# Prefix sums on the diagonal of a 2D prefix sum: two column groups moved from TensorE to VectorE, an early fp32 load, and smaller last pieces

## The chip, the cores and the metric

One core of one Trainium2 chip. The metric is device time in microseconds (us). The kernel before takes 668.2 us (median of 6 runs, 667.48 to 669.82).

## The reference

```python
def setup_inputs():
    B, H, W = 4, 4224, 4224
    return {"x": np.random.randn(B, H, W).astype(np.float32)}

def reference(x):
    ps = np.cumsum(np.cumsum(x, axis=1), axis=2)
    diag = np.diagonal(ps, axis1=1, axis2=2)
    return np.cumsum(diag, axis=1).astype(np.float32)
```

Output n is the sum, over diagonal positions up to n, of everything above and left of that position. Every element is read once: 285 MB of fp32 (the page has 285.47 MB read), which the loads cast to bf16 on the way into SBUF (142.47 MB as the software queue wrote them).

## The kernel before

Rows come in strips of 768 (6 per partition) through three buffers. Columns are cut into 11 groups of 384. For a strip, TensorE adds up the columns right of the diagonal block (matmuls with a one-hot column, into `d`), VectorE masks the diagonal block and adds up rows left of it, ScalarE takes a share of those. In the first three batches VectorE adds up one group instead in four of the strips (`by_rows`, result in `rowed`). `rows` are the sums per row; a matmul that reads them adds them to `d`, along which VectorE then runs two scans (prefix sums). A fold is a run of matmuls with the identity, which adds up column pieces on TensorE. The granted clock is the share of TensorE's full clock that the trace records. Cuts are marked `# ...`.

```python
head = last.tile([P, 2, HC], FP32, name="head")          # HC = 528
nc.sync.dma_start(out=head, in_=src_a[:, :, N - HC : N])  # before all strips
# ...
def add_up(strip, f, r0, acc, um, wp=0, ws=None, by_rows=False):
    # ...
    for j in range(g + nw + by_rows, NG):
        for q in range(f):
            columns(j, 0, GW, strip[:, q, j * GW : (j + 1) * GW], q > 0)
    # ...
    nc.vector.tensor_mul(out=mu, in0=block, in1=um)
    nc.vector.tensor_sub(out=block, in0=block, in1=mu)
    if by_rows:
        rowed = mup.tile([P, GW], FP32, name="rowed")
        row_sums(rowed, strip[:, :, hi : hi + GW].rearrange("p q c -> p c q"))
    # ... matmuls on mu, and one on rowed
    row_sums(acc[:, :, 1], strip[:, :, ws:hi])
# ... the last batch ends in two three-row strips, 256 rows (part_a), then
# 128 rows (part_b) in pieces of 32, the last of these in two pieces:
for sb, c0, c1 in ((0, 0, CB), (1, 0, CB), (2, 0, CB), (3, 0, bcut), (3, bcut, CB)):
    nc.gpsimd.dma_start(out=part_b[:, sb, c0:c1], in_=...)
# ... per piece a sum on ScalarE and one on VectorE (pair_sum), weighed by TensorE
pair_sum(esum[:, 1:2], part_b[:, 3, 320:bcut])
pair_sum(esum[:, 2:3], part_b[:, 3, bcut:])
# ...
nc.vector.tensor_add(out=ye, in0=fin_e, in1=yl[:, E0:])
nc.sync.dma_start(out=out[b, T0 + E0 : N].unsqueeze(0), in_=ye)
```

## Time and profile before

| | before |
|---|---|
| span of the profiled run | 665.6 us |
| TensorE, VectorE, ScalarE busy | 206.6, 380.8, 136.1 us |
| loads that go through the software queue | 142.47 MB as written, 99.9% of 16 engines' span |
| instruction fetches of 16 KB | 7 |
| last strip landed (TensorE starts on it) | 648.81 us |
| last sum on VectorE starts | 662.69 us |

The table's first four rows are the profile page; the last two are start times in the timeline. The lines themselves are in the prediction. Where this text speaks of single DMA packets (their queue, size, start and duration), these are records of the trace that no view prints; an engine is recognised in them only by its back-to-back packets, it has no name.

### The profile page before, as it was taken

The page shows a single profiled execution, that of the slowest core. Times are in us where ns is not written, and L with a number is a line of the kernel's source. Part 1 is how long each engine was busy: PE and PEld are TensorE (multiplying, and loading weights), DVE is VectorE, ACT ScalarE, POOL GpSimd, SP SyncE. Part 2 cuts the span into 40 slices and gives each one's busy share as a digit, 9 for nine tenths or more (in the row PEclk, how much of TensorE's full clock was granted, in tenths as well). Part 3 has the DMA queues.
Part 4 walks back from the last instruction along what each step waited for, and adds up shares of the span by engine and source line. Part 5 has one row for each costly group of instructions (what it writes and reads, how often), then busy time and mean ns, then how long its engine had stood idle before and what let it go on. Part 6 is the DMA issues. An engine that isn't in the chain of part 4 may idle for free.

```text
span 665.6 us, 2495 instructions
## 1 busy us (share of the span) xinstructions
PE 206.6 (31%) x948; PEld 94.1 (14%) x948; DVE 380.8 (57%) x176; ACT 136.1 (20%) x219; POOL 31.3 (5%) x59
## 2 busy tenths in 40 slices
PE   0071522302117143140211723404031363350418
PEld 0030211100003021010000311201000131120103
DVE  3161828476946173756794526466589433352766
ACT  0001121406300103040630020304063002030434
POOL 7000000000000000000000000000000000001000
PEclk9995857656558585665655857657565585776758
DMA  9999999999999999999999999999999999999998
GB/s 203 219 219 219 219 219 218 218 209 210 219 220 219 218 220 219 218 216 215 209 219 219 219 216 219 219 218 216 213 213 219 219 216 216 219 218 218 215 206 162
DMA packets 7672, 143.23 MB, mean 215 GB/s; under 512 B 704, under 2 KB 1004, under 8 KB 2156
## 3 DMA queue, kind: packets, MB, share of 16 engines
q0 software_dynamic: 7296, 142.47, 99.9%
q1 hardware_dynamic: 364, 0.61, 0.3%
q8 instruction: 7, 0.11, 0.1%
q14 instruction: 5, 0.04, 0.0%
HBM read 285.47 MB, written 0.07 MB: 429 GB/s over the span
## 4 chain that ended last, share of the span: by engine, by line
DVE 54%; another core or an unknown queue 37%; DMA 5%; PE 3%; issue 1%; DVEq 0%; POOLq 0%
DVE acc L258 28%; DVE mu L351 8%; DVE strip L352 8%; DVE rowed L258 7%; DMA strip<-in_x_dram 5%; DVE c L481 1%; PE d L211 1%; PE fold L218 0%; PE d L218 0%; DVE pu L258 0%; DVE c L278 0%; DVE rows L403 0%; DVE acc L376 0%; PE fold_a L218 0%
## 5 line engine op out<-in xcount | busy, mean ns | idle before, releaser
L253 ACT ACTIVATE dump<-strip 128x416 bf16<-128x416 bf16 (+6 forms) x108 | 124.4, 1151 | 520.2 <-DMA strip<-in_x_dram 517.5
L351 DVE TENSOR_TENSOR mu<-strip,um 128x4608 bf16<-128x4608 bf16 (+1 forms) x24 | 52.4, 2184 | 260.4 <-DMA strip<-in_x_dram 260.3
L258 DVE TENSOR_REDUCE acc<-strip 128x6 f32<-128x4608 bf16 (+6 forms) x23 | 195.9, 8518 | 0.4
L218 PEld LDWEIGHTS <-sel 128*11 128x11 bf16 x643 | 66.7, 104 | 482.5 <-issue 453.6
L211 PE MATMUL d<-strip,sel 128*11 128x384 bf16 x90 | 37.3, 415 | 295.8 <-DMA strip<-in_x_dram 295.8
L218 PE MATMUL d<-strip,sel 128*11 128x384 bf16 x441 | 116.6, 408 | 0.0
L352 DVE TENSOR_TENSOR strip<-strip,mu 128x4608 bf16<-128x4608 bf16 (+1 forms) x24 | 52.4, 2183 | 1.0
L211 PE MATMUL d<-mu,sel 128*11 128x384 bf16 x43 | 16.3, 379 | 108.5 <-DVE mu L351 108.5
L258 DVE TENSOR_REDUCE rowed<-strip 128x384 f32<-128x2304 bf16 x12 | 49.0, 4082 | 0.0
L218 PE MATMUL d<-mu,sel 128*11 128x384 bf16 x200 | 46.7, 369 | 0.0
L76 POOL DMA_DIRECT2D strip<-in_x_dram x24 | 16.4, 686 | 542.7 <-DVE acc L258 292.8
L253 ACT ACTIVATION_READ_ACCUMULATOR dump<-strip 128x1 f32 x108 | 20.1, 186 | 0.0
L211 PE MATMUL d<-rowed,sel_f 128*11 128x384 f32 x24 | 11.5, 566 | 20.3 <-DVE rowed L258 20.3
L211 PEld LDWEIGHTS <-sel 128*11 128x11 bf16 x134 | 13.6, 102 | 19.3 <-issue 12.3
L211 PE MATMUL d<-ident,rows 128*11 128x128 f32 x24 | 5.2, 379 | 16.8 <-DVE rows L412 16.8
L258 DVE TENSOR_REDUCE pu<-d 11x1 f32<-11x384 f32 x4 | 2.2, 545 | 6.3 <-PE d L211 6.3
L94 DVE MEMSET um<- 128x4608 bf16 (+1 forms) x2 | 4.9, 2458 | 1.1 <-issue 1.1
L95 POOL TENSOR_SCALAR_AFFINE_SELECT um<-um 128x4608 bf16<-128x4608 bf16 (+1 forms) x2 | 5.2, 2612 | 2.6 <-DVE um L94 2.6
L211 PE MATMUL d<-halves,rows 128*11 128x64 f32 x48 | 5.3, 288 | 0.0
L211 PEld LDWEIGHTS d<-ident,rows 128*11 128x11 f32 x24 | 2.5, 118 | 18.9 <-DVE rows L412 11.7
L211 PEld LDWEIGHTS d<-rowed,sel_f 128*11 128x11 f32 x24 | 1.5, 91 | 24.9 <-DVE rowed L258 24.6
L211 PEld LDWEIGHTS d<-halves,rows 128*11 128x11 f32 x48 | 4.8, 128 | 1.4 <-issue 1.3
(102 smaller groups left out, 60.6 us busy)
## 6 DMA issues: line engine op xcount, KB each, us to landing
strip<-in_x_dram POOLq DMA_DIRECT2D x19, 6336.0 KB, 72.6
strip<-in_x_dram POOLq DMA_DIRECT2D x5, 3168.0 KB, 55.8
strip<-in_x_dram POOLq DMA_DIRECT2D x1, 1080.0 KB, 49.9
strip<-in_x_dram POOLq DMA_DIRECT2D x1, 768.0 KB, 52.9
strip<-in_x_dram POOLq DMA_DIRECT2D x3, 256.0 KB, 54.1
head<-in_x_dram SPq DMA_DIRECT2D x1, 528.0 KB, 3.8
strip<-in_x_dram POOLq DMA_DIRECT2D x1, 192.0 KB, 43.2
strip<-in_x_dram POOLq DMA_DIRECT2D x1, 64.0 KB, 28.5
```

Of the source, the lines that this page charges most:

```text
L76: nc.gpsimd.dma_start(out=o, in_=x[b, r0 : r0 + f * P, :].rearrange("(p f) w -> p f w", f=f))
L94: nc.vector.memset(um, 1.0)
L95: nc.gpsimd.affine_select(out=um, in_=um, compare_op=ALU.is_gt, fill=0.0, base=0, pattern=[[-1, f], [1, f * P]], channel_multiplier=-f,)
L211: nc.tensor.matmul(o, lhsT=lhsT, rhs=rhs, start=start, stop=False, skip_group_check=True)
L218: te.add_instruction(mybir.InstMatmult(start_tensor_calc=False, stop_tensor_calc=False, tile_position=(0, 0), tile_size=(P, P if lhsT.shap ...
L253: nc.scalar.activation(out=dump[:, :w], in_=src, func=ACT.Copy, accum_out=acc)
L258: nc.vector.reduce_sum(out=acc, in_=src, axis=AX.X)
L351: nc.vector.tensor_mul(out=mu, in0=block, in1=um)
L352: nc.vector.tensor_sub(out=block, in0=block, in1=mu)
L481: nc.vector.tensor_tensor_scan(out=c12[:, i, :], data0=ones_row, data1=src, initial=carry[:, i : i + 1], op0=ALU.mult, op1=ALU.add,)
```

## The change

Its intent: (1) take the two rightmost groups, 9 and 10, off TensorE for all six-row strips: VectorE adds them up in one fp32 tile per batch (a wide add has 768 columns, a narrow one, in the fifth strip of the first three batches, 384), so that TensorE reads only two fp32 tiles per batch; (2) make the end shorter: half of the last 16 rows is loaded right after `head`, before all strips, with an access pattern of outer size 8 meant for 8 DMA engines, and the last loads are three pieces of 131 KB of fp32; (3) issue the store of the groups after the next one. The core of the diff:

```diff
+    early = last.tile([P, EC], FP32, name="early")          # RE = 16, EC = 256
+    nc.sync.dma_start(out=early,
+        in_=src_e.rearrange("(a b) (k c) -> a b k c", b=2, k=EK)[:, :, :, :EC])
...
-            for j in range(g + nw + by_rows, NG):
+            for j in range(g + nw, RJ if right else NG):     # RJ = NG - 2
...
-            if by_rows: rowed = ...; row_sums(rowed, ...)    # and its matmul
+            if right:                                        # after row_sums(acc)
+                c0 = max(hi, RJ * GW)
+                to = right_cols[:, c0 - RJ * GW :]
+                for q in range(f):
+                    if r0 == 0 and q == 0:
+                        continue
+                    nc.vector.tensor_add(out=to,
+                        in0=to if r0 + q > 1 else strip[:, 0, c0:],
+                        in1=strip[:, q, c0:])
...
-            add_up(..., um6, by_rows=whole and s > 0)
+            add_up(..., um6, right=True)
...
+        for j in range(RJ, NG):
+            matmul(d, sel_f[...], right_cols[:, (j - RJ) * GW : (j - RJ + 1) * GW])
...
-   (3, 0, bcut), (3, bcut, CB)
+   for i, (src, c) in enumerate(((src_e, EC), (src_l, 0), (src_l, EC))):
+       nc.gpsimd.dma_start(out=late[:, i * EC : (i + 1) * EC], in_=src...[:, :, c : c + EC])
...
+        store_groups()      # now after the store of yl; one shared tile for pair_sum
```

## The prediction

> **What bounds the kernel now.** I read the slices of the page first, then the waits, the chain in order of time, and last the timeline of the final 30 us.
>
> ```profile
> DVE  3161828476946173756794526466589433352766
> DMA  9999999999999999999999999999999999999998
> GB/s 203 219 219 219 219 219 218 218 209 210 219 220 219 218 220 219 218 216 215 209 219 219 219 216 219 219 218 216 213 213 219 219 216 216 219 218 218 215 206 162
> ```
>
> The 16 DMA engines are busy in nine tenths of every slice but the last, VectorE (DVE) in no long stretch. The kernel is one stream of loads. The waits, where the columns are total us, times and the longest, agree:
>
> ```profile
> POOL strip L76 <- DVE acc L258: 292.8, 9, 35.3
> ...
> DVE mu L351 <- DMA strip<-in_x_dram: 260.3, 20, 20.0
> ```
>
> VectorE waits 260 us for strips. GpSimd (POOL) waits for VectorE to free a buffer, but with three buffers that costs nothing: in the chain (start, us, what) six-row strips reach VectorE every 29.9 us, and it is done some 7 to 20 us before the next.
>
> ```profile
> 454.24 2.57 DVE mu L351
> 456.83 2.56 DVE strip L352
> 459.39 4.00 DVE rowed L258
> 463.39 11.26 DVE acc L258
> 474.65 9.39 another core or an unknown queue
> 484.09 0.04 issue
> 484.13 2.57 DVE mu L351
> ```
>
> The trace's records of single DMA packets say why the stream can't be hurried: a 25344-byte strip packet takes 1886 ns on its engine, and the next starts 1867 ns after it. So only three things count: work per DMA engine, what lies idle at the start, and what follows the last landing. The end of the timeline (start, us, engine, line, operation) is therefore the part to know:
>
> ```profile
> 624.12 11.35 DVE L258 TENSOR_REDUCE acc<-strip 128x6 f32<-128x10752 bf16 x1
> ...
> 635.58 0.18 DVE L376 TENSOR_TENSOR acc<-acc 128x24 f32<-128x24 f32 x1
> ...
> 643.63 0.17 DVE L420 COPY rows<-acc 128x3 f32<-128x3 f32 x1
> ...
> 648.86 0.76 DVE L351 TENSOR_TENSOR mu<-strip,um 128x1152 bf16<-128x1152 bf16 x1 [5.05 <-DMA strip<-in_x_dram]
> ...
> 654.47 0.17 DVE L258 TENSOR_REDUCE rows<-parts 128x3 f32<-128x9 f32 x1
> ...
> 655.36 0.83 PE L211 MATMUL d<-ident,rows 128*11 128x128 f32 x6
> ...
> 658.88 1.00 DVE L481 TENSOR_TENSOR_SCAN c<-ones_row,carry,c 11x384 f32<-11x384 f32 x1
> ...
> 662.35 0.39 DVE L267 SCALAR_TENSOR_TENSOR pair<-strip 128x224 f32<-128x224 bf16 x1
> ...
> 662.69 0.29 DVE L267 SCALAR_TENSOR_TENSOR pair<-strip 128x128 f32<-128x128 bf16 x1
> ```
>
> From 648.86 VectorE works almost without a pause: its only slack ahead of the end is 5.05 us before the last strip, and 0.72 us on TensorE (PE) between rows (done 654.64) and the matmul that reads it (655.36), which stands behind a fold. The last load's completion writes go out at 661.95 to 662.35 and the last pair_sum starts at 662.69, so DMA and VectorE end nearly together.
>
> [...] the 64-column fp32 add at L137 took 225 ns [...], the bf16 multiply of 4608 columns 2558 ns [...]. [...] The trace names no engine, but the 10-row store did go out as 10 packets. [...] each engine's first strip packet starts at 3.74 to 4.27 us, right as its last packet of head ends.
>
> **Part 1, groups 9 and 10 on VectorE.** Removed: 12 reductions `rowed` of 4.08 us, 49.0 us. Added: [...] A batch has 5+6+6+6 = 23 wide ones, the first three batches 6 narrow ones as well. [...] VectorE goes from 380.8 to about 430 us. TensorE loses 138 of 531 strip matmuls (instruction lists of both), at 0.41 us 57 us. In mid-stream neither shows: the busiest strip takes VectorE 5.1 + 11.3 + 6.0 = 22.4 us of 29.9. In the last batch, though, nothing is removed, since `rowed` was not used there. Its fourth strip now ends at 635.54 + 6.0 = 641.5. The three-row strip after it took from 635.58 to 643.80, 8.2 us, so it ends at 649.8, and VectorE meets the last strip (648.86) 0.9 us late. rows is then done at 655.55, the matmul starts 0.14 us later (the lag in earlier batches: 187.07 to 187.21), at 655.68 for 655.36. Of 0.9 us, 0.3 come through. From there to the last pair_sum VectorE is a chain.
>
> **Part 2, early load and last pieces.** All engines lose 8 packets of 1536 B (0.119 us apart) and 8 of 512 B (0.045) and gain 24 of 512 B and one completion of 0.02: 1.31 us to 1.10, -0.2 us at the end. Eight engines gain 16 packets of 1 KB fp32, an estimated 0.042 us each from 2112 B in 0.082: +0.7 us. As head already keeps each engine busy until its first strip packet, this is not hidden at the start; it is hidden only on engines that end early. In the packet records seven end by about 661.3 and nine at 662.0 to 662.35; the slow ones each appear to have carried a 16 KB instruction fetch (0.95 us). Of the ten packets of the row store four go out only at 661.97 to 662.31, on late engines. [...] There the end moves by -0.2 + 0.7 = +0.5 at worst, by +0.1 for the earliest of them. If fetches fall elsewhere in the changed kernel, it is -0.2.
>
> **Part 3, the rest.** The later store removes one 0.08 us packet from an engine's tail at most. The first of the last pieces to VectorE shrinks from 0.39 to 0.29 us; one shared pair tile makes each wait for the one before, about +0.08. These cancel. The sums for weights and earlysum fall in the idle first 34 us.
>
> **Sum.** VectorE's chain ends +0.3 us, the loads between -0.2 and +0.5; the later counts: about +0.3 on 668.14, so 668.4.
>
> **Rivals.** (a) The loads alone set the end, and the early bytes are hidden on the fast engines: -0.2 to -0.3 us, 667.9. For it: the intent, and DMA at nine tenths. Against: VectorE's last start is set by its own predecessor as closely as by the landing. (b) The early load sits on late engines and pushes every landing: +0.5, 668.6. For it: the four late store packets. Against: no record names the engine. (c) VectorE becomes the bound: 50 us more, buffers come free late, the stream stalls, several us (675). Against: at least 7 us idle remain per strip, and a freed buffer's load queues behind a whole other strip. (d) The 57 us less of TensorE speed the kernel: no, it waits 296 us for strips.
>
> **Range and chances.** The terms are tenths of a us; the three runs before span 0.7 us, and another chip or another placing of fetches can add as much. So 667.4 to 669.2. 2% is 13.4 us, which nothing here reaches: faster 0.01, same 0.98, slower 0.01.
>
> **What would show it.** Right: wide adds near 0.96 us; VectorE near 430 us busy; TensorE near 150; strips 29.9 us apart; VectorE meeting the last strip some 0.9 us late with no wait before it; scans and the last pair_sum some 0.3 us later than before. Wrong: a wait before the last strip's multiply (adds cheaper than reckoned), a last landing that moves by over 0.6 us either way, or strips further apart, which would mean that buffers come free too late.

## The result, and the profile after

The changed kernel takes 668.48 us (median of 6, 667.85 to 670.04), the kernel before in the same rounds 668.2. The ratio is 1.0005 with a 95% interval of 0.999 to 1.0021. Here and below a ratio is the mean time of one kernel's fast runs over that of the other's fast runs in the same rounds, so it is not quite the ratio of the medians. The times alone do not settle the sign.

The slices of the page, for the changed kernel, show the same stream of loads with a fuller VectorE (431.0 us busy):

```profile
DVE  3280929486948193857793827476689463765896
DMA  9999999999999999999999999999999999999998
```

The groups by form (line, engine, operation, tiles, shapes, count, then busy us and mean ns of one) have the adds at 957 and 556 ns:

```profile
L396 DVE TENSOR_TENSOR right_cols<-right_cols,strip 128x768 f32<-128x768 f32 x88 | 84.2, 957 | 2.6
L396 DVE TENSOR_TENSOR right_cols<-right_cols,strip 128x384 f32<-128x384 f32 x18 | 10.0, 556 | 0.5
```

In mid-stream the chain (start, us, what) still has 7 us of waiting behind the longest strip:

```profile
471.78 0.88 DVE right_cols L396
472.65 0.02 issue
472.68 0.97 DVE right_cols L396
...
477.61 7.07 another core or an unknown queue
484.68 0.03 issue
```

And the end of the timeline:

```profile
635.99 5.92 DVE L396 TENSOR_TENSOR right_cols<-right_cols,strip 128x768 f32<-128x768 f32 x6
...
649.36 0.36 PE L237 MATMUL fold<-strip,ident_h 128*128 128x480 bf16 x1 [2.38 <-DMA strip<-in_x_dram]
649.95 0.76 DVE L380 TENSOR_TENSOR mu<-strip,um 128x1152 bf16<-128x1152 bf16 x1
...
655.56 0.17 DVE L284 TENSOR_REDUCE rows<-parts 128x3 f32<-128x9 f32 x1
655.78 0.83 PE L237 MATMUL d<-ident,rows 128*11 128x128 f32 x6 [0.38 <-DVE rows L284]
...
663.14 0.29 DVE L294 SCALAR_TENSOR_TENSOR pair<-strip 128x128 f32<-128x128 bf16 x1
```

The six adds of the last batch's fourth strip are there, 5.92 us where 6.0 was reckoned. VectorE takes up the last strip (649.95) with no wait in front, 0.59 us after it landed (649.36, when TensorE starts on it). The strip itself landed 0.55 us later than before. The matmul that reads `rows` comes 0.42 us later than before and now waits for VectorE. The last sum is 0.45 us later, the last store's issue 0.42 (664.03 for 663.61). With the one shared pair tile the last sum starts 0.04 us after the end of the one before it (662.81 + 0.29 to 663.14); with a tile each it started 0.05 us ahead of that end (662.35 + 0.39 to 662.69).

So two things moved by half a us: the landings, and VectorE against the landing. The experiments ask which of them the end pays for, and how much of it is scatter.

### The profile page after: what moved, and what is told of

Its sections match the earlier page's. It is cut to its first block, busy times and chain, and to the rows that moved or that the text cites. A ratio compares the mean times of both kernels' runs of the same rounds, so it can differ in the third digit from the quotient of the medians.

```text
span 666.4 us, 2314 instructions
## 1 busy us (share of the span) xinstructions
PE 180.7 (27%) x804; PEld 81.7 (12%) x804; DVE 431.0 (65%) x279; ACT 136.1 (20%) x219; POOL 32.1 (5%) x62
## 4 chain that ended last, share of the span: by engine, by line
DVE 57%; another core or an unknown queue 27%; DMA 13%; issue 1%; PE 1%; POOL 0%; ACT 0%; DVEq 0%; POOLq 0%; ACTq 0%
DVE acc L284 27%; DVE right_cols L396 14%; DMA strip<-in_x_dram 13%; DVE mu L380 7%; DVE strip L381 7%; DVE c L517 1%; PE d L237 1%; DVE pu L284 0%; DVE c L305 0%; POOL strip L474 0%; POOL strip L478 0%; DVE rows L441 0%; ACT dump L279 0%; DVE acc L409 0%
## 5 line engine op out<-in xcount | busy, mean ns | idle before, releaser
L244 PEld LDWEIGHTS <-sel 128*11 128x11 bf16 x528 | 56.3, 107 | 457.4 <-issue 435.7
L237 PE MATMUL d<-strip,sel 128*11 128x384 bf16 x67 | 28.7, 428 | 308.4 <-DMA strip<-in_x_dram 308.4
L396 DVE TENSOR_TENSOR right_cols<-right_cols,strip 128x768 f32<-128x768 f32 (+1 forms) x106 | 94.2, 889 | 3.2
L244 PE MATMUL d<-strip,sel 128*11 128x384 bf16 x326 | 89.4, 420 | 0.0
L244 PE MATMUL d<-mu,sel 128*11 128x384 bf16 x200 | 49.8, 388 | 0.0
L237 PE MATMUL d<-mu,sel 128*11 128x384 bf16 x43 | 16.7, 389 | 82.0 <-DVE mu L380 82.0
L237 PE MATMUL d<-right_cols,sel_f 128*11 128x384 f32 x16 | 10.9, 793 | 59.6 <-DVE right_cols L396 59.6
L237 PEld LDWEIGHTS <-sel 128*11 128x11 bf16 x111 | 11.6, 105 | 25.1 <-issue 19.3
L237 PEld LDWEIGHTS d<-right_cols,sel_f 128*11 128x11 f32 x16 | 1.5, 114 | 65.5 <-DVE right_cols L396 63.6
```

Source lines behind the costliest of these rows:

```text
L237: nc.tensor.matmul(o, lhsT=lhsT, rhs=rhs, start=start, stop=False, skip_group_check=True)
L244: te.add_instruction(mybir.InstMatmult(start_tensor_calc=False, stop_tensor_calc=False, tile_position=(0, 0), tile_size=(P, P if lhsT.shap ...
L396: nc.vector.tensor_add(out=to, in0=to if r0 + q > 1 else strip[:, 0, c0:], in1=strip[:, q, c0:],)
```

## The experiments

**Theory:** the loads set the pace; the early load costs at the start about what it takes off the end; VectorE's six extra adds make it late for the last strip and pass a few tenths on. **Rivals:** the loads alone matter; VectorE alone matters; it is all scatter of single executions.

This table has what each trace shows. First column of numbers: mean start of the 16 engines' first strip packets. Second: mean end of their last full strip packets. Third: last strip landed. Fourth: from there to the matmul that reads `rows`. Fifth: last completion write of a load. Sixth: start of the last pair sum. All in us; the first, second and fifth are from the packet records, the others from the timeline. Each row is one execution. The runs with experiments were made in three sets, each on one chip: adds_only, early_only, last_on_pe and dose_tail on chip 9; before_again, hc384, early16 and dose_mid on chip 5; before_warm and after_again on chip 15. The ratios compare runs of one set, the rows of the table mix them.

| kernel | first packets | strips end | last strip | to rows matmul | last load | last sum |
|---|---|---|---|---|---|---|
| before | 3.96 | 647.78 | 648.81 | 6.55 | 662.35 | 662.69 |
| before_again | 3.95 | 647.80 | 648.71 | 7.06 | 662.29 | 663.01 |
| before_warm | 4.06 | 648.01 | 649.63 | 5.96 | 663.20 | 663.53 |
| hc384 | 3.73 | 648.01 | 649.65 | 7.04 | 663.52 | 663.92 |
| adds_only | 3.94 | 647.90 | 649.27 | 6.37 | 662.78 | 663.24 |
| early_only | 4.25 | 648.09 | 648.98 | 6.04 | 662.25 | 662.68 |
| last_on_pe | 4.37 | 648.18 | 649.63 | 6.57 | 662.94 | 663.57 |
| after | 4.41 | 648.18 | 649.36 | 6.42 | 662.67 | 663.14 |
| after_again | 4.35 | 647.95 | 648.96 | 7.12 | 662.26 | 664.30 |
| early16 | 4.35 | 648.15 | 649.24 | 6.42 | 662.55 | 663.02 |
| dose_mid | 4.34 | 648.01 | 649.22 | 6.43 | 662.54 | 663.12 |
| dose_tail | 4.34 | 648.63 | 651.20 | 10.48 | 664.51 | 670.49 |

### The adds alone

The kernel before with the diff's adds and nothing else (three pair tiles instead of four, for room).

```diff
-            add_up(..., by_rows=whole and s > 0)
+            add_up(..., right=True)
```

> The kernel before, plus the right-column adds alone (no early load, old last pieces, old store). Theory 1 (VectorE's extra 6 us on the fourth strip of the last batch makes it late for the last strip, the loads unchanged): fourth and last strip land as before (first TensorE use at 618.9 and 648.8 us), VectorE's multiply on the last strip starts 0.9 us later than 648.86, the last pair sum starts 0.3 us later than 662.69; time +0.3 us (ratio 1.0005). Rival (the early load alone makes the loss): multiply and pair sum as before, ratio 1.000.

Measured: 667.77 us for 667.36 of the kernel before, ratio 1.0006 (0.9994 to 1.0019). VectorE is late for the last strip without any early load:

```profile
649.82 0.76 DVE L352 TENSOR_TENSOR mu<-strip,um 128x1152 bf16<-128x1152 bf16 x1
655.42 0.16 DVE L259 TENSOR_REDUCE rows<-parts 128x3 f32<-128x9 f32 x1
655.64 0.83 PE L212 MATMUL d<-ident,rows 128*11 128x128 f32 x6 [0.37 <-DVE rows L259]
```

The multiply starts at 649.82, 0.96 us later than before, as expected; but the strip landed 0.46 us later too, which the theory did not expect. The rows matmul is 0.28 us later than before. The last sum is 0.55 us later, where 0.3 was expected; the last load was 0.43 us later as well. So the adds do make VectorE late, and landings move by 0.4 us in a kernel with no extra load.

### The early load, the last pieces and the later store alone

```diff
-            add_up(..., right=True)
+            add_up(..., by_rows=whole and s > 0)     # and no right_cols
```

> The changed kernel with the old row reductions in place of the adds (early load, new last pieces and later store kept). Theory 1: every strip lands 0.3 to 0.6 us later than in the kernel before, VectorE waits for the last strip as before (some 5 us), the last landing is 0.1 to 0.4 us later, and the time +0.1 to +0.4 us. Rival (the loads at the start are hidden, the tail is shorter): strips land as before, last landing 0.2 us earlier, time -0.2 us.

Measured: 668.07 us, ratio 1.0016 (1.0003 to 1.0028). First packets are 0.29 us later, the last strip 0.17 us later than in the kernel before, VectorE waits 5.02 us for it:

```profile
649.03 0.76 DVE L379 TENSOR_TENSOR mu<-strip,um 128x1152 bf16<-128x1152 bf16 x1 [5.02 <-DMA strip<-in_x_dram]
654.64 0.16 DVE L283 TENSOR_REDUCE rows<-parts 128x3 f32<-128x9 f32 x1
655.02 0.83 PE L236 MATMUL d<-ident,rows 128*11 128x128 f32 x6
```

The last load is 0.10 us earlier than before and the last sum starts within 0.01 us of before. So the expectation was missed at the end (0.1 to 0.4 us later): in this execution the early load cost nothing there; the five timed runs were 0.16% slower all the same. The rival (hidden at the start, 0.2 us gained) fails at its first step, as the strips do start later.

### The adds kept out of the last batch

```diff
-            add_up(..., right=True)
+            add_up(..., right=whole)
...
-        for j in range(RJ, NG):
+        for j in range(RJ, NG) if whole else ():
```

> The changed kernel with groups 9 and 10 of the last batch left to TensorE (no adds there). Theory 1: VectorE waits some 4 to 5 us for the last strip again, though strips still land 0.3 to 0.6 us late; the last pair sum is bound by the last landing; time within 0.3 us of the changed kernel, -0.1 expected. Rival (VectorE's lateness is all of the loss): time back to that of the kernel before.

Measured: 668.53 us, ratio 1.0016 (1.0004 to 1.0029), no gain. VectorE waits for the last strip again:

```profile
649.68 0.76 DVE L380 TENSOR_TENSOR mu<-strip,um 128x1152 bf16<-128x1152 bf16 x1 [5.00 <-DMA strip<-in_x_dram]
655.29 0.16 DVE L284 TENSOR_REDUCE rows<-parts 128x3 f32<-128x9 f32 x1
656.20 0.83 PE L237 MATMUL d<-ident,rows 128*11 128x128 f32 x6
```

Yet the rows matmul comes 0.91 us after `rows`, so TensorE is what was late here. Against expectation, the last sum was not bound by the last load (662.94) but by this chain. VectorE's lateness, then, is not what separates the changed kernel from a faster one: take it away and TensorE takes its place.

### A dose of VectorE at the end, and in mid-stream

In dose_tail one more reduction of 3840 columns, its result unused, follows the adds of the last batch's fourth strip; in dose_mid it follows those of all 15 six-row strips of the first three batches.

```diff
+                if not whole and r0 == 3 * F2 * P:      # dose_tail; "if whole:" in dose_mid
+                    row_sums(spare, strip[:, 0, :3840])
```

> The changed kernel with one more reduction of 3840 columns (4.1 us, result unused) on VectorE after the adds of the fourth strip of the last batch. Theory 1: no slack is left there, so VectorE meets the last strip 4.1 us later still (about 4.7 us late), and the end moves by about +4.1 us, ratio to the kernel before 1.0065. Rival (the loads alone set the end): the end moves by under 1 us.

> The changed kernel with the same unused reduction of 3840 columns (4.1 us) added to every six-row strip of the first three batches, 15 in all, 62 us of VectorE. Theory 1 (mid-stream VectorE work is free while a strip's total stays under 29.9 us; here 26.6): strips still 29.9 us apart, time within 0.3 us of the changed kernel. Rival (buffers come free too late, VectorE's share matters): time longer by several us.

dose_mid: 668.32 us, ratio 1.0005 (0.9991 to 1.002), as the changed kernel. VectorE's busy time rises by 61 us to 491.9 us and the time not at all. Its chain at the longest strip with adds of full width shows the dose eating the wait:

```profile
477.05 4.06 DVE spare L284
481.11 3.43 another core or an unknown queue
484.64 2.57 DVE mu L380
```

dose_tail: 674.35 us, ratio 1.0099 (1.0083 to 1.0114), some 6 us above the changed kernel where 4.1 was expected. VectorE meets the last strip 4.66 us late (655.86 against 651.20), as reckoned. The profiled execution has two additions: its strips landed late (fourth strip 621.39 for 619.54, the latest engine ended its strips 1.5 us behind the next), and TensorE, which now waits 2.94 us for `rows`, comes back at half clock. In the stretches (start:end, length, busy us and count of TensorE, its weight loads, VectorE, ScalarE, GpSimd, then granted clock, DMA share and GB/s):

```profile
658.00:661.00 3.00, 0.74 (x3) 0.12 (x3) 3.00 (x2) 0.00 (x0) 0.00 (x0) 1.00 1.14 208
661.00:662.00 1.00, 0.32 (x2) 0.24 (x3) 0.53 (x2) 0.00 (x0) 0.00 (x0) 0.75 1.02 151
662.00:664.00 2.00, 2.00 (x9) 0.80 (x8) 0.82 (x2) 0.00 (x0) 0.00 (x0) 0.50 0.28 39
```

From the rows matmul to the last sum it takes 8.81 us (661.68 to 670.49) against 7.36 in the changed kernel (655.78 to 663.14), 1.45 us more. 4.1 + 1.45 is 5.6; in the profiled execution the last strip's later landing (1.84 us) comes on top. So work is free in mid-stream and paid in full after the fourth strip of the last batch, once VectorE's slack there is used up.

### The kernels before and after, profiled once more

> The kernel before, unchanged, profiled again, to see how far its landings move from execution to execution. Theory 1: the same instruction fetches, engines' first strip packets at 3.7 to 4.3 us with a mean within 0.1 us of 3.96, last strip landed within 0.5 us of 648.8. Rival (the shifts of 0.3 to 0.6 us seen so far are mere scatter): the mean of the first packets moves by 0.3 us or more.

> The changed kernel, unchanged, profiled again for scatter. Theory: mean start of strip packets 4.25 to 4.45 us, rows matmul 6.4 us after the last strip's landing (set by VectorE, so the same within 0.1 us in every kernel with the adds), last strip landed between 649.0 and 649.7. Rival (the first profile was an odd one): any of these off by more.

before_again (667.57 us) repeats the fetches, the first packets (3.95) and the last strip (648.71). The shift of the first packets in every kernel with the early load, 0.3 to 0.45 us, is therefore no scatter, and it shows on each of the three chips (chip 9: 4.25, 4.37 and 4.34 for 3.94; chip 5: 4.35 and 4.34 for 3.95; chip 15: 4.35 for 4.06). But one thing moved: the rows matmul came 7.06 us after the landing instead of 6.55, although `rows` was ready earlier:

```profile
653.88 1.21 PE L211 MATMUL d<-halves,rows 128*11 128x64 f32 x12
...
654.37 0.16 DVE L258 TENSOR_REDUCE rows<-parts 128x3 f32<-128x9 f32 x1
...
655.77 0.83 PE L211 MATMUL d<-ident,rows 128*11 128x128 f32 x6
```

The `halves` matmuls took 1.21 us for 0.83 before. In both executions TensorE's granted clock was 0.50 from 649 to 653 us, after a pause of some 10 us, and came back to full within 653 to 655 (mean there 0.83 before, 0.59 here). In the kernel before TensorE, not VectorE, sets the rows matmul, and how late depends on when its clock comes back.

after_again (669.29 us) broke the expectation: 7.12 us from landing to rows matmul, not 6.4. Here TensorE had its clock early, was done early, and had to wait 2.23 us for part_a. The stretches:

```profile
652.00:653.00 1.00, 0.48 (x9) 0.40 (x7) 1.00 (x1) 0.97 (x3) 0.00 (x0) 1.00 1.06 216
653.00:654.00 1.00, 0.00 (x0) 0.00 (x0) 1.00 (x1) 0.79 (x2) 0.00 (x0) 1.00 1.06 206
654.00:655.00 1.00, 0.29 (x1) 0.10 (x1) 1.00 (x2) 0.00 (x0) 0.00 (x0) 0.86 1.09 215
655.00:656.00 1.00, 1.00 (x3) 0.15 (x1) 0.21 (x2) 0.00 (x0) 0.00 (x0) 0.50 1.04 206
```

The clock falls to half just as the folds and the rows matmul are to run. The last sum starts at 664.30, 1.16 us later than in the first profile, though the last load landed 0.41 us earlier. That is where this execution's extra us came from.

The fall comes right after the pause of 2.23 us. The length of a pause alone does not settle it, though. In the same execution an earlier pause of 3.04 us (645.92 to 648.96) left the clock at 1.00, as did one of 3.13 us in early16, while 2.10 us ahead of the last strip in adds_only cost it. The trace's clock records and TensorE's instructions, put side by side, show a difference. As counted in the twelve traces, all 466 stretches between two changes of the clock, those at the two ends of a trace left out, are whole multiples of 3.41 us. After 282 such steps at full clock it stayed, and TensorE had been busy for at least 0.42 of the step; after 232 it fell, and in all but one (0.52) the busy share was at most 0.41. From half clock it came back after 234 steps, all busy for at least 0.77. In the two traces of the kernel before and the changed kernel alone these are 84 stretches; 46 steps kept full clock (busy for 0.43 or more), 42 lost it (0.41 or less) and 42 regained it (0.77 or more). The 2.23 us lie in one step (651.31 to 654.73); the 3.04 us are cut by a step's edge at 647.90 into 1.98 and 1.06.

### TensorE kept warm in the kernel before

```diff
+            for _ in range(2):
+                fold_in(fold_g, strip[:, :F], 0, 3200, 160, start=True)   # unused
             fold_in(fold_g, strip[:, F:], 0, wp, 160, start=True)
```

> The kernel before with 40 unused 480-column matmuls on TensorE in its 10 us pause ahead of the last strip (they write a sum that the next start overwrites). Theory: in the kernel before, TensorE at half clock and not VectorE sets the matmul that reads rows, 6.0 to 7.1 us after the last strip's landing; warm, the folds run at 0.2 us instead of 0.4 and the matmul comes 5.9 to 6.0 us after the landing, where VectorE sets it. The end gains at most 0.3 us, as the last load lands at 662.3 either way. Rival (TensorE's clock plays no part, VectorE's chain sets it): the same 6.5 us or more, time unchanged.

Measured: 668.06 us for 667.77, ratio 1.0003 (0.9988 to 1.0018). The clock is 1.00 from 644 us on, the folds take 1.58 us instead of 3.00, and the rows matmul follows the landing by 5.96 us, set by VectorE. Both as expected:

```profile
649.83 1.58 PE L218 MATMUL fold<-strip,ident_h 128*128 128x480 bf16 x7
...
655.59 0.83 PE L211 MATMUL d<-ident,rows 128*11 128x128 f32 x6
```

The end gains nothing: in this execution the last load ended at 663.20, where 662.3 was expected, and VectorE waited 0.40 us for it. This was also the only candidate for a version faster than both, and it does not come out faster.

### The start

> The kernel before with the first load of head narrowed from 528 to 384 columns (0.147 MB moved from the start to the late rows piece, on all 16 engines alike). Theory 1 (no idle time at the start beyond the first packet's latency: work moved to the start costs as much there): strip packets start some 0.3 us earlier (mean 3.6), the last landing is unchanged, time within 0.2 us of before. Rival (the start hides loads for free [...]): strip packets start as before at 3.9 on average, last landing 0.35 us later.

```diff
-    HC = 528
+    HC = 384
```

> The changed kernel with the early load on 16 DMA engines [...] instead of 8. Theory 1 (engine work is conserved): each engine's strips start 0.3 to 0.4 us late instead of 0.7 on eight; mean start of strip packets 4.3 to 4.4 as in the changed kernel; latest engine within 0.4 us of the changed kernel's, time within 0.3 us. Rival (eight engines were the cause of the late landings): last strip and last landing 0.3 to 0.5 us earlier than in the changed kernel, time -0.3 us or more.

```diff
-        in_=src_e.rearrange("(a b) (k c) -> a b k c", b=2, k=EK)[:, :, :, :EC],
+        in_=src_e.rearrange("r (k c) -> r k c", k=EK)[:, :, :EC],
```

hc384, 0.147 MB less at the start: first packets at 3.73 instead of 3.96 (3.6 was expected), so they follow the end of head, and the rival (a start that hides loads for free) falls. The time was 669.53 us for 667.96, ratio 1.0014 (1.0001 to 1.0027), where no change was expected: two runs at 667.6 and 668.4, four at 669.5 to 669.7. In the profiled run (668.44) one engine finished its share of the first strip at 35.98 us, 1.87 us behind the next, and the last engine's strips end at 649.30. Why one engine starts late in some executions stays open.

early16: 668.04 us for 667.96, ratio 1.0002 (0.999 to 1.0014); first packets and landings within 0.13 us of the changed kernel's. But this run compared nothing. The packet records of SyncE's hardware queue have small writes of 4 bytes that close a transfer, and their number shows how many engines it ran on: the one-row stores have 1 each, `head` has 16. The kernel before has 62 in all (16 for `head`, 11, 11, 11 and 10 for the stores of the groups, 3 for the three one-row stores). The changed kernel and early16 both have 78. The early load thus ran on 16 engines in the changed kernel too, whatever its access pattern says, and 12 of its 16 engines start their strips between 4.29 and 4.51 us, not in two groups 0.7 us apart. A load on 8 engines was never measured.

## Why the prediction was right

The time predicted was 668.4 us, measured 668.48, and no 2% either way. That no 2% would come followed from the mechanism; that the number is met within 0.1 us is luck, since six runs span 2.2 us and two of the steps (the engines of the early load, TensorE at the end) were not as described. By its own steps:

- **Loads bound the kernel; mid-stream work is free.** Right, and shown by dose_mid: 61 us more on VectorE cost nothing.
- **Wide adds near 0.96 us; VectorE near 430 us.** Right: 957 ns for the wide and 556 for the narrow adds, 431.0 us. The predicted length was the author's estimate. One from the profile before alone comes close: its bf16 multiplies (L351) took 759 ns for 1152 columns and 2558 for 4608, so 0.52 ns a column and 159 ns besides; if the fp32 add of 64 columns at L137, 225 ns, has the same 159 in it, it took 1.03 ns a column, which makes 0.95 us for 768 columns and 0.55 for 384.
- **TensorE down by 57 us to about 150.** Wrong: 180.7 us. The step multiplied 138 matmuls by their mean duration of 0.41 us, but these overlap: the strip groups' busy time before was 37.3 + 116.6 = 153.9 us for 531, 0.29 each, and it fell by 35.8 us. TensorE as a whole fell by 25.9 us. It weighed nothing in the sum.
- **VectorE late for the last strip by 0.9 us.** The mechanism was right (no wait ahead of the multiply; in adds_only it starts 0.96 us later than before). Against the landing it was 0.59 us in the changed kernel, because the strip itself came 0.55 us later.
- **0.3 us of it comes through.** The two profiles of the changed kernel and of before give 655.78 and 656.08 against 655.36 and 655.77 for the rows matmul, so +0.4 us between the means of two executions each. But the step's reason was incomplete. It took TensorE's 0.72 us of slack as fixed; it is TensorE at clock 0.50 after a 10 us pause, and ranges from 6.0 (early_only) to 7.1 us from the landing. With the adds VectorE sets 6.4 us, when TensorE is done in time. So VectorE's lateness lies beside a TensorE chain of about the same length, as last_on_pe confirms.
- **Early load: not hidden, +0.7 us on eight engines; -0.2 us at the end.** Not hidden is shown: first packets 0.3 to 0.45 us later on average in every kernel that has it. The eight engines were wrong: the load ran on all sixteen (see early16), with 8 packets of 46 ns and a completion write of about 0.01 us on each, 0.38 us where 0.7 or nothing was reckoned. So the argument from late engines, and the 10 packets of the row store as a sign of it, fall away (a store of 11 rows has 11 packets: one per row). By the prediction's own figures each engine then has 0.38 - 0.2, about 0.2 us more to do; this too is less than VectorE's 0.3, so the sum would have stayed. At the end of the strips the average engine is 0.2 to 0.4 us behind the kernel before in all six profiles with the early load and no dose at the end, but so it is, by 0.1 to 0.2 us, in adds_only, before_warm and hc384, which don't have it; the last load moved by -0.1 to +0.6 us, and by +0.4 to +1.2 us in those three. The saving of 0.2 us at the end is not shown by any run.
- **Late engines carry an instruction fetch.** Supported in the packet records of the kernel before: engines that finish a strip about a us behind the rest number one after the first fetch (71 us), then two, three, four and five after those at 195, 264, 374 and 458. A fetch took 0.89 to 0.97 us of one engine in the kernels before and after, 0.89 to 1.03 over all profiles. Every kernel with the adds has 6 fetches, every other one 7; the latest engine is as far behind as ever (strips end 1.6 us apart, 1.4 before; 1.2 to 2.1 in all profiles but dose_tail, which has 3.1).
- **The rivals.** (c), a stalled stream, is refuted by dose_mid (a six-row load lands 72.6 us after its issue, by the median of the page before, with strips 29.9 us apart); for (d) nothing speaks, as adds_only, with 27.5 us less of TensorE, is not faster. The premise of (b), an early load on some engines only, falls with the sixteen. Between (a) and the sum the times can't decide: the four readings of kernels with the early load and no dose (early_only, last_on_pe, early16, after) lie between 1.0002 and 1.0016.

Shown, then: why the change gains nothing. What it takes from TensorE was free, what it puts on VectorE is free but for the last strip, and the early load makes the first strip packets start 0.3 to 0.45 us later. Whether the smaller end makes up for this shift can't be read from the last loads, whose scatter is larger than the terms. Not settled: whether the exact sum is 0 or +0.3 us, and how often an engine starts late or TensorE's clock drops at the end, the two things seen to add a us or more to single executions.

## What to carry to other kernels

Where loads fill nine tenths of every slice, ask what an engine's work costs before the last landings and after: a dose of known length in mid-stream and one at the end tell it in two runs (here 61 us in mid-stream cost nothing, 4.1 us at the end cost some 6). A load moved to the start is not free by its place alone: here the early load made the first big packets 0.3 to 0.45 us later. Look at when they begin, and whether they move when the first small load shrinks (3.96 to 3.73 us in hc384). In the last microseconds TensorE's granted clock went with its pauses and with where they fell (0.50 after one of 2.23 us, 1.00 after one of 3.04, both in after_again), so a faster step ahead of it can make it wait, lose its clock and end later, as there (7.12 us from landing to rows matmul for 6.42). And before a run is said to compare two placements, look in the trace whether the two differ (early16: 78 closing writes in both).
